# Modulation products and low halves of weights: from VectorE and GpSimd to VectorE alone, in two mixers

## The chip, the cores and the metric

The program runs on one core of a Trainium2 chip, in one launch. The metric is the device time of that launch in microseconds (us). The page and the rows below name the engines as the profiler does: PE is TensorE's matmul stream and PEld its weight loads, DVE is VectorE, ACT is ScalarE, POOL is GpSimd, and SP (SyncE) issues the loads from HBM.

## The reference, cut to what matters

Two blocks of layers work on 256 tokens of width 1024. The first has two layers, the second one; each layer is a mixer (attention or a scan) and an MLP, each followed by a normalised residual. In the first block both are modulated by vectors that a projection of the condition `c` gives:

```python
c_act = jax.nn.silu(c)
for l in range(DEPTH):                                   # 2 layers
    ada = c_act @ ada_w[l] + ada_b[l]                    # 1024 -> 6 * 1024
    sh1, sc1, g1, sh2, sc2, g2 = jnp.split(ada, 6, axis=-1)
    h = modulate(x, sh1, sc1)
    y = even_mixer(h, ...) if l % 2 == 0 else diff_mixer(h, ...)
    x = layer_norm(ALPHA * x + (1.0 + g1[:, None, :]) * y, ...)
    h = modulate(x, sh2, sc2)
    y = sq_relu_mlp(h, mlp_w1[l], mlp_w2[l])
    x = layer_norm(ALPHA * x + (1.0 + g2[:, None, :]) * y, ...)
```

`even_mixer` is the first mixer: a block-compressed attention (8 heads with compressed, selected and window keys) and a latent attention with an index score that keeps the best 64 keys. `diff_mixer` is the second. The third mixer, in the second block, joins a gated delta rule (a convolution, normalised keys, a scan over chunks of 64 tokens) and a grouped attention with 16 meta tokens. All is in float32.

## The kernel before, in words

Weights. All weights lie in one array `in_ws`, in tiles of 128 partitions by up to 1024 float32 (512 KB). Each product with a weight is made of three matmuls on halves of the mantissa, `mm3` (L385 to L389): the weight's high part `hi` is a rounded copy that ACT makes from the raw tile (`cast_hi`, L346 and L347), its low part `lo` is `raw - hi` (`cast_lo`, L349 to L352). SP issues every load, in the order of the program (`load_raw`, L333 to L337). The raw tiles stand in a ring of seven slots in both places that this change touches; SP can issue the next load once the last reader of the oldest slot is done.

Modulation. A vector of the modulation has 1024 entries, in eight parts of 128. For each part `ada_dot` (L451) loads a raw tile of 128 by 1024 on SP (L457) and needs the sum over its 1024 columns of tile times `cact`. There are two forms. With `pool` false it is one instruction of DVE, a product with a running sum (L478), and the reading of the accumulator. With `pool` "half" POOL multiplies the tile's first 512 columns by `cact` in place (L461), at the next step its other 512, and at the step after ACT runs over all 1024 columns and sums them (L474).

First mixer (`layer0`, L1036 on). Its work is a list of weight pieces (matmuls), beside a set of generators ("chains") that hold attention's steps; `weave` (L1957) goes round: each chain one step, then the casts that are due, then a piece. Three vectors of the modulation (24 dots) are one of the chains, `weave_ada` (L1070 to L1090), which starts at the 17th round and makes three steps of a dot in the POOL form and two of one in the DVE form. Here the vectors (0, 2), (0, 4) and (0, 3) are all in `spread`, so that the dots with an even part, 12 of 24, take the POOL form. In this mixer only ACT works in the order in which the program is written (`MAN[0]` is 'A'); for DVE, POOL and PE the tile scheduler sets the order.

Third mixer (`mixer2`, L2007 on). It calls the same `weave` twice. In the first call (L2029) the low part of the weights is cut by `share`, here `SHARE2` = 8: the first eight weights that the round casts have their whole low part on DVE; from the ninth on DVE makes columns 0 to 511 and POOL columns 512 to 1023. There are 11 such weights. In the second call `share` is 0, and all its weights are cut so. ACT and DVE work in written order in the first call ('AD'), in the second POOL too.

The names that come up below: `se` is a softmax tile, scaled on POOL at L1457; `ol` at L1234 are POOL's products of the compressed values; `isc` at L1163 are the index scores of the latent attention, summed over heads on DVE; `selneg` at L1189 is the mask that the selection of the best keys ends with; `C` at L2267 and `zn` at L2599 are tiles of the third mixer's scan and gate.

Of the kernel before, what the change touches and what calls it, by code (L numbers as in the profile page):

```python
# [29 lines left out]
ADA0 = 16  # L30
# [3 lines left out]
MORE1 = 2  # L34
SHARE1 = None
SHARE0 = None
SHARE2 = 8
MAN = ['A', 'ADG', 'AD', 'ADG', 'P']
EARLY = {1: "tok0", 3: "tok1", 5: "tok2", 6: "tok3"}
LAM_INIT = 0.8 - 0.6 * math.exp(-0.3)  # L40
# [226 lines left out]
class Kern:  # L267
# [768 lines left out]
    def layer0(self, stop):  # L1036
        nc, ph = self.nc, self.ph
        st = self.st = SimpleNamespace(tok=False, cmp=0, sel=0, lat=False, pc=False, scored=0)
        self.F, self.part, self.oh, self.L0 = {}, {}, None, None
        self.blk = self.T(self.acts, (128, 16, 64), "ol")  # L1040
        nc.gpsimd.memset(self.blk, 0.0)
        self.blkw = self.T(self.acts, (128, 16, 128), "oh", F32R)
        self.tok = self.T(ph, (128, 2, 416), "tok")
        self.hs = self.T(ph, (128, 256), "isc", bufs=3)
        work = []
        for n in ORDER0.split():
            f = (lambda wh, wl, i=int(n[-1]): self.tok0(i, wh, wl)) if n[:3] == "tok" else \
                (lambda wh, wl, n=n[4], i=int(n[5]): self.cmp0(n, i, wh, wl)) if n[:3] == "cmp" else \
                (lambda wh, wl, n=n: self.fm0(n, wh, wl))
            work.append((n if n[:3] == "cmp" else f"ev_{n}", None, f))  # L1050

        def begin(half):
            return half == 0 or st.scored == 4

        self.merged = set()
        work += self.out_work("ev_out", range(4), lambda k: (self.oh[:, k, :], self.ol[:, k, :]),
                              self.merged.__contains__, range(4, 4 + MORE0), begin)
        units = [self.nsa0(j) for j in range(4)] + [self.dsa0(i) for i in range(4)]
        chains = [self.loads0(), self.tok0_after(), self.compress0(), self.compressed0(), self.latent0(), self.queue(units),
                  *(self.merge0(j) for j in range(8)), self.select0(), self.weave_ada((0, 2), (0, 4), (0, 3), start=ADA0, spread=((0, 2), (0, 4), (0, 3)))]  # L1060
        self.weave(work, chains, share=SHARE0)
        self.in_order = False
        if stop == "attn0":
            for j in range(8):
                t = self.T(ph, (128, 256), "dbgo", bufs=1)
                nc.vector.tensor_add(t, self.oh[:, j, :].bitcast(F32), self.ol[:, j, :].bitcast(F32))
                self.dump(f"oT{j}", t)
        return stop != "attn0"
# [938 lines left out]
    def mixer2(self, ph, stop):  # L2007
# [7 lines left out]
        with self.banks(a=1, b=1, c=1, d=1), tc.tile_pool(name="wv", bufs=1, side="right") as wv:  # L2015
# [12 lines left out]
                      self.attn2_queries(wv, zq, aq, qT), self.delta_meta(ph, wv), att, self.gate2(wv, zz)]  # L2028
            left = self.weave(work, chains, (att,), share=SHARE2, man=2)  # L2029
        self.ctx2.enter_context(self.room(4, 3, "right"))  # L2030
# [725 lines left out]
```

## Time and profile before

| | |
|---|---|
| time, median of 3 runs | 1166.39 us (1165.0 to 1170.65) |
| the profiled execution | 1162.97 us |
| its span | 1161.2 us |
| granted clock of TensorE, mean | 0.955 |
| PE busy | 1073.1 us, 92% of the span |
| DVE busy | 840.5 us, 72% |
| ACT busy | 595.3 us, 51% |
| POOL busy | 269.3 us, 23% |
| the chain that ended last, by engine | PE 68%, DVE 14%, DMA 5%, POOL 5%, issue 4%, ACT 3% |

The first mixer lies from about 46 to 200 us of the span, the first call of `weave` in the third mixer ends at about 882 us. The shares in the table are means over stages of different kinds: the profile's 40 slices show POOL busy only in the stages of the mixers and DVE busiest in those of the first and third. "Idle before, with a releaser" in a row means that the engine stood still ahead of the instruction, and what event ended that. Busy times of one instruction include whatever it waited for once it had begun, so that the same shape can have different durations.

### The profile page before, as it was taken

What the parts mean: (1) busy time and instruction counts of PE and PEld (TensorE: products, weight loads), DVE (VectorE), ACT (ScalarE), POOL (GpSimd) and SP (SyncE); (2) the same over time, 40 slices, a digit from 0 to 9 for tenths busy, and PEclk for the clock granted to TensorE, in tenths of its full rate; (3) what the DMA queues carried; (4) which work ended last, traced back from release to release, by engine and by line L of the source; (5) the groups of instructions that cost most, each with busy time, mean ns of one, the idle gap of its engine ahead of it and who ended that gap; (6) DMA issues with size and microseconds to landing.
All of it is one profiled execution on the core that took longest, in us unless ns stands there. A gap on an engine that the chain in (4) does not pass through costs nothing.

```text
span 1161.2 us, 20465 instructions
## 1 busy us (share of the span) xinstructions
PE 1073.1 (92%) x7766; PEld 975.4 (84%) x7766; DVE 840.5 (72%) x1672; ACT 595.3 (51%) x1240; POOL 269.3 (23%) x307
## 2 busy tenths in 40 slices
PE   2789889999999999997999999998899989999996
PEld 1667667999999978896999999887776888899995
DVE  7578985799886677877976555678986677655553
ACT  2456747464445445653754444557365354544442
POOL 3284673100000201324000000336644250000000
PEclk9799888999999989997999999899899997999998
DMA  9977643299996227636587553032120252765621
GB/s 344 316 266 271 210 155 112 89 404 349 331 336 229 97 90 294 211 135 235 202 287 237 183 179 119 1 109 92 55 66 27 92 200 68 252 189 182 189 83 37
DMA packets 60447, 212.58 MB, mean 183 GB/s; under 512 B 6619, under 2 KB 9084, under 8 KB 60348
## 3 DMA queue, kind: packets, MB, share of 16 engines
q1 hardware_dynamic: 59424, 209.43, 51.3%
q0 software_dynamic: 192, 0.79, 0.4%
q8 instruction: 61, 1.00, 0.3%
q10 hardware_dynamic: 732, 1.05, 0.3%
q14 instruction: 38, 0.31, 0.1%
HBM read 209.15 MB, written 1.84 MB: 182 GB/s over the span
## 4 chain that ended last, share of the span: by engine, by line
PE 68%; DVE 14%; DMA 5%; POOL 5%; issue 4%; ACT 3%; POOLq 0%; DVEq 0%; ACTq 0%; SPq 0%
PE y L387 10%; PE y L388 10%; PE y L389 10%; PE pj L387 7%; PE pj L389 7%; PE pj L388 7%; DMA raw<-in_ws 3%; PE tr L392 2%; DVE lo L352 2%; PE y L401 2%; DVE raw L478 1%; PE y L392 1%; PE pj L392 1%; DVE cva L2178 1%; POOL se L1457 1%
## 5 line engine op out<-in xcount | busy, mean ns | idle before, releaser
L366 DVE TENSOR_TENSOR lo<-raw,hi 128x1024 fp32r<-128x1024 f32 (+1 forms) x208 | 226.6, 1105 | 107.0 <-ACT hi L365 106.9
L365 ACT ACTIVATE hi<-raw 128x1024 fp32r<-128x1024 f32 (+1 forms) x208 | 195.3, 959 | 94.1 <-PE pj L388 76.4
L387 PE MATMUL pj<-hh,hi 128*128 128x256 f32 x768 | 216.7, 282 | 0.3
L388 PE MATMUL pj<-hl,hi 128*128 128x256 f32 x768 | 216.6, 282 | 0.2 <-DVE hl L611 0.2
L389 PE MATMUL pj<-hh,lo 128*128 128x256 f32 x768 | 215.7, 281 | 0.0
L352 DVE TENSOR_TENSOR lo<-raw,hi 128x1024 fp32r<-128x1024 f32 (+2 forms) x103 | 126.6, 1236 | 42.2 <-ACT hi L347 40.8
L387 PEld LDWEIGHTS pj<-hh,hi 128*128 128x128 f32 x768 | 145.1, 189 | 2.5 <-ACT relu L807 0.9
L388 PEld LDWEIGHTS pj<-hl,hi 128*128 128x128 f32 x768 | 144.9, 189 | 1.6 <-DVE hl L611 0.4
L389 PEld LDWEIGHTS pj<-hh,lo 128*128 128x128 f32 x768 | 145.2, 189 | 0.0
L388 PE MATMUL y<-actl,hi 128*128 128x256 f32 x512 | 144.3, 282 | 0.8 <-DVE actl L810 0.7
L387 PE MATMUL y<-acth,hi 128*128 128x256 f32 x512 | 144.0, 281 | 0.0
L389 PE MATMUL y<-acth,lo 128*128 128x256 f32 x512 | 143.7, 281 | 0.0
L352 POOL TENSOR_TENSOR lo<-raw,hi 128x512 fp32r<-128x512 f32 (+3 forms) x28 | 47.5, 1703 | 357.9 <-ACT hi L347 335.9
L347 ACT ACTIVATE hi<-raw 128x1024 fp32r<-128x1024 f32 (+2 forms) x107 | 110.8, 1043 | 27.1 <-DMA raw<-in_ws 16.1
L478 DVE CUSTOM_DVE_ANT_0 raw<-raw,cact 128x1024 f32<-128x1024 f32 x75 | 97.1, 1303 | 2.7 <-DMA raw<-in_ws 2.7
L388 PEld LDWEIGHTS y<-actl,hi 128*128 128x128 f32 x512 | 96.9, 189 | 1.5 <-DVE actl L810 1.4
L387 PEld LDWEIGHTS y<-acth,hi 128*128 128x128 f32 x512 | 97.1, 190 | 0.1
L389 PEld LDWEIGHTS y<-acth,lo 128*128 128x128 f32 x512 | 96.8, 189 | 0.0
L388 PE MATMUL y<-hl,hi 128*128 128x256 f32 x296 | 84.5, 286 | 0.0
L387 PE MATMUL y<-hh,hi 128*128 128x256 f32 x264 | 79.7, 302 | 3.9 <-ACT f L1588 2.2
L809 ACT ACTIVATE acth<-act 128x256 fp32r<-128x256 f32 x96 | 39.4, 416 | 83.5 <-DVE act L808 83.5
L389 PE MATMUL y<-hh,lo 128*128 128x256 f32 x264 | 76.8, 291 | 0.0
(658 smaller groups left out, 2486.3 us busy)
## 6 DMA issues: line engine op xcount, KB each, us to landing
raw<-in_ws SPq DMA_DIRECT2D x372, 512.0 KB, 4.7
bm<-bscr SPq DMA_DIRECT2D x4, 512.0 KB, 14.6
raw<-in_ws SPq DMA_DIRECT2D x4, 416.0 KB, 8.7
bm<-in_ws SPq DMA_DIRECT2D x3, 512.0 KB, 8.2
raw<-in_ws SPq DMA_DIRECT2D x3, 408.0 KB, 3.7
zn<-in_ws SPq DMA_DIRECT2D x2, 512.0 KB, 6.6
xa<-in_xT SPq DMA_DIRECT2D x2, 512.0 KB, 6.6
oh<-in_ws SPq DMA_DIRECT2D x2, 512.0 KB, 7.3
```

Of the source, the lines that this page charges most:

```text
L347: return self.nc.scalar.activation(w[1], w[0], AF.Copy)
L352: return eng.tensor_tensor(w[2][:, a:b], w[0][:, a:b], w[1][:, a:b].bitcast(F32), op=OP.subtract)
L365: i = nc.scalar.activation(hi[:, a:b], raw[:, a:b], AF.Copy)
L366: j = (lo_by or nc.vector).tensor_tensor(lo[:, a:b], raw[:, a:b], hi[:, a:b].bitcast(F32), op=OP.subtract)
L387: mm(out, lh, rh, start=start, stop=False, skip_group_check=True)
L388: mm(out, lh, rl, start=False, stop=False, skip_group_check=True)
L389: mm(out, ll, rh, start=False, stop=stop, skip_group_check=True)
L392: self.nc.tensor.matmul(out, l, r, start=start, stop=stop, skip_group_check=True)
L401: last = self.nc.tensor.matmul(out, l, r, start=start, stop=stop, skip_group_check=True)
L478: nc.vector.tensor_tensor_reduce(out=raw, in0=raw, in1=self.cact, op0=OP.mult, op1=OP.add, scale=0.5, scalar=0.0, accum_out=t)
L809: nc.scalar.activation(ah, f, AF.Copy)
L1457: nc.gpsimd.tensor_scalar(es[g][:, sl], es[g][:, sl], sm[:, tb, g:g + 1], 1.0, op0=OP.mult, op1=OP.mult)
```

## The change

Two lines are changed. `SHARE2` becomes `None`, which `weave` reads as "no weight is cut": the 11 weights of the first call in the third mixer have their whole low part on DVE, in one instruction of 128 by 1024. And `weave_ada` is called without `spread`, whose default is empty: all 24 dots of the first mixer take the DVE form.

```diff
-SHARE2 = 8
+SHARE2 = None
...
         chains = [self.loads0(), self.tok0_after(), self.compress0(), self.compressed0(), self.latent0(), self.queue(units),
-                  *(self.merge0(j) for j in range(8)), self.select0(), self.weave_ada((0, 2), (0, 4), (0, 3), start=ADA0, spread=((0, 2), (0, 4), (0, 3)))]
+                  *(self.merge0(j) for j in range(8)), self.select0(), self.weave_ada((0, 2), (0, 4), (0, 3), start=ADA0)]
```

In the instruction streams SP's order is the same. ACT loses the 12 sums of L474 and nothing else moves on it. POOL loses 24 products of L461 and 11 low halves of L352. DVE gains 12 dots of L478 with their accumulator reads, and 11 casts of L352 grow from 512 to 1024 columns.

DVE in the first mixer, about a third of the way through it: in the rows, `raw` and `lo` with a number are the tile of a weight or of a dot, `adas` the dot's result, `oh` a merge of compressed values. Before:

```order
L352 TENSOR_TENSOR lo_161_720<-raw_159_717,hi_160_719 128x1024
L1239 TENSOR_TENSOR oh_271<-ol_269,oh_271 128x16x32
L352 TENSOR_TENSOR lo_172_765<-raw_170_762,hi_171_764 128x1024
L478 ISA raw_180_817,adas_505<-raw_180_817,cact_87 128x1024
L478 ISA adas_505 128x1
L352 TENSOR_TENSOR lo_178_802<-raw_176_799,hi_177_801 128x1024
L1163 SCALAR_TENSOR_TENSOR isc_684<-hfull_683,iw_363,p_l_90_401 128x256
```

And now:

```order
L352 TENSOR_TENSOR lo_161_716<-raw_159_713,hi_160_715 128x1024
L1239 TENSOR_TENSOR oh_271<-ol_269,oh_271 128x16x32
L478 ISA raw_174_774,adas_505<-raw_174_774,cact_87 128x1024
L478 ISA adas_505 128x1
L478 ISA raw_180_809,adas_505<-raw_180_809,cact_87 128x1024
L478 ISA adas_505 128x1
L352 TENSOR_TENSOR lo_172_759<-raw_170_756,hi_171_758 128x1024
L352 TENSOR_TENSOR lo_178_795<-raw_176_792,hi_177_794 128x1024
L1163 SCALAR_TENSOR_TENSOR isc_682<-hfull_681,iw_363,p_l_90_401 128x256
```

The dot of tile 174, which POOL made before, now stands on DVE, and it and the dot of tile 180 both stand ahead of the low parts of the weights 172 and 178 and of the first index score.

POOL at the same stage, where `se` are softmax tiles and `ol` the compressed products. Before:

```order
L461 TENSOR_TENSOR raw_141_637<-raw_141_637,cact_87 128x512 x2
L1457 TENSOR_SCALAR se_538<-se_538,ssum_540 128x128
L1457 TENSOR_SCALAR se_538<-se_538,ssum_540 128x256
L1457 TENSOR_SCALAR se_539<-se_539,ssum_540 128x128
L1457 TENSOR_SCALAR se_539<-se_539,ssum_540 128x256
L1234 TENSOR_TENSOR ol_269<-c_578,p_l_90_401 64x16x15 x2
L461 TENSOR_TENSOR raw_166_738<-raw_166_738,cact_87 128x512 x2
L1234 TENSOR_TENSOR ol_269<-c_661,p_l_90_401 64x16x15 x2
L1457 TENSOR_SCALAR se_623<-se_623,ssum_625 128x128
```

And now:

```order
L1234 TENSOR_TENSOR ol_269<-c_576,p_l_90_401 64x16x15
L1457 TENSOR_SCALAR se_538<-se_538,ssum_540 128x128
L1457 TENSOR_SCALAR se_538<-se_538,ssum_540 128x256
L1457 TENSOR_SCALAR se_539<-se_539,ssum_540 128x128
L1457 TENSOR_SCALAR se_539<-se_539,ssum_540 128x256
L1234 TENSOR_TENSOR ol_269<-c_576,p_l_90_401 64x16x15
L1234 TENSOR_TENSOR ol_269<-c_659,p_l_90_401 64x16x15 x2
L1457 TENSOR_SCALAR se_621<-se_621,ssum_623 128x128
```

The two pairs of products no longer stand ahead of the softmax's scalings and of the compressed products.

DVE in the third mixer, at the ninth weight that the round casts, among steps of the scan (`Cd`, `cvo`, `tokk`). Before:

```order
L2278 TENSOR_TENSOR Cd_9400<-C_9342,bd_8910 128x256
L2183 SCALAR_TENSOR_TENSOR cvo_9382<-cvo_9382,cva_9264 128x272
L352 TENSOR_TENSOR lo_1794_9392<-raw_1792_9389,hi_1793_9391 128x512
L2255 TENSOR_TENSOR tokk_8932<-tm_9310,nkr_9349 128x256
L2249 COPY mk_8930<-cvo_9382 128x2x16
```

And now:

```order
L2278 TENSOR_TENSOR Cd_9376<-C_9318,bd_8886 128x256
L2183 SCALAR_TENSOR_TENSOR cvo_9358<-cvo_9358,cva_9240 128x272
L352 TENSOR_TENSOR lo_1794_9368<-raw_1792_9365,hi_1793_9367 128x1024
L2255 TENSOR_TENSOR tokk_8908<-tm_9286,nkr_9325 128x256
L2249 COPY mk_8906<-cvo_9358 128x2x16
```

Nothing changes place; the cast covers twice the columns, and the half on POOL is gone.

## Rows read from the trace of the kernel before

**Rows 1.** Busy time by stretch: us, PE, PEld, DVE, ACT, POOL, granted clock, DMA share, GB/s.
```profile
60.00:92.00 32.00, 27.30 (x168) 21.25 (x168) 20.98 (x35) 18.63 (x44) 26.26 (x24) 0.89 0.60 218
92.00:160.00 68.00, 62.65 (x429) 50.34 (x428) 64.33 (x169) 47.57 (x115) 39.27 (x41) 0.95 0.70 247
...
790.00:850.00 60.00, 48.44 (x362) 46.40 (x360) 56.36 (x124) 32.25 (x80) 40.09 (x47) 0.94 0.22 71
850.00:882.00 32.00, 30.14 (x209) 24.27 (x209) 25.77 (x78) 19.61 (x58) 12.64 (x16) 1.00 0.21 67
```

**Rows 2.** POOL's groups, 92 to 160 us: busy us, mean ns, idle before.
```profile
L461 POOL TENSOR_TENSOR raw<-raw,cact 128x512 f32<-128x512 f32 x14 | 24.5, 1766 | 15.6 <-DVE lo L352 6.7 <-DMA raw<-in_ws 5.5 <-DVE smin L1444 3.3
```

**Rows 3.** DVE's groups, 92 to 160 us.
```profile
L352 DVE TENSOR_TENSOR lo<-raw,hi 128x1024 fp32r<-128x1024 f32 x17 | 25.3, 1493 | 8.0 <-ACT hi L347 8.0
L478 DVE CUSTOM_DVE_ANT_0 raw<-raw,cact 128x1024 f32<-128x1024 f32 x8 | 11.5, 1434 | 0.0
L1163 DVE SCALAR_TENSOR_TENSOR isc<-hfull,iw,isc 128x256 f32<-128x256 f32 x7 | 6.3, 899 | 0.0
L1444 DVE CUSTOM_DVE_ANT_0 se<-y,bm 128x256 f32<-128x256 f32 x12 | 4.9, 412 | 0.0
...
L1163 DVE SCALAR_TENSOR_TENSOR isc<-hfull,iw,p_l 128x256 f32<-128x256 f32 x1 | 1.5, 1495 | 0.0
```

**Rows 4.** Line L1163 alone, 92 to 160 us: shortest, median and longest ns.
```profile
L1163 DVE SCALAR_TENSOR_TENSOR isc<-hfull,iw,isc x14: 338/408/1523, 97.7 to 118.8; 128x256 f32<-128x256 f32 x7, 128x128 f32<-128x128 f32 x7
```

**Rows 5.** DVE's groups, 226 to 390 us.
```profile
L366 DVE TENSOR_TENSOR lo<-raw,hi 128x1024 fp32r<-128x1024 f32 x54 | 65.4, 1221 | 16.1 <-ACT hi L365 16.1
L478 DVE CUSTOM_DVE_ANT_0 raw<-raw,cact 128x1024 f32<-128x1024 f32 x32 | 38.3, 1216 | 0.0
L478 DVE DVE_READ_ACCUMULATOR2_ANT adas<- 128x1 f32 x32 | 2.6, 80 | 0.0
```

**Rows 6.** Timeline of POOL, 69 to 112 us: start, us, instruction, idle before.
```profile
78.31 3.40 POOL L461 TENSOR_TENSOR raw<-raw,cact 128x512 f32<-128x512 f32 x2
81.67 2.46 POOL L1234 TENSOR_TENSOR ol<-c,p_l 64x240 f32<-64x240 f32 x2
...
102.87 3.74 POOL L461 TENSOR_TENSOR raw<-raw,cact 128x512 f32<-128x512 f32 x2 [5.21 <-DVE lo L352]
```

**Rows 7.** Timeline of DVE, three pieces between 84 and 160 us.
```profile
91.59 1.22 DVE L352 TENSOR_TENSOR lo<-raw,hi 128x1024 fp32r<-128x1024 f32 x1 [6.00 <-ACT hi L347]
...
103.19 4.50 DVE L352 TENSOR_TENSOR lo<-raw,hi 128x1024 fp32r<-128x1024 f32 x2
...
159.07 0.23 DVE L1189 TENSOR_SCALAR selneg<-isc 128x128 f32<-128x128 f32 x1
```

**Rows 8.** Timeline of ACT, 83 to 92 us.
```profile
84.16 0.63 ACT L1237 ACTIVATE oh<-ol 128x512 fp32r<-128x512 f32 x1 [3.69 <-POOL ol L1234]
...
89.47 1.05 ACT L474 ACTIVATE raw<-raw 128x1024 f32<-128x1024 f32 x1
```

**Rows 9.** Waits of SP, 46 to 200 us: us in total, times, longest.
```profile
SPq L336 <- ACT raw L474: 13.9, 4, 4.8
SPq L457 <- ACT raw L474: 11.3, 2, 7.5
```

**Rows 10.** DVE's and POOL's groups, 790 to 850 us.
```profile
L2267 DVE SCALAR_TENSOR_TENSOR C<-ol,beta,C 128x128 f32<-128x128 f32 x6 | 5.8, 962 | 0.2
L352 DVE TENSOR_TENSOR lo<-raw,hi 128x512 fp32r<-128x512 f32 x7 | 5.0, 713 | 0.2 <-ACT hi L347 0.2
...
L352 POOL TENSOR_TENSOR lo<-raw,hi 128x512 fp32r<-128x512 f32 x8 | 10.8, 1345 | 0.5 <-ACT hi L347 0.4
```

**Rows 11.** Timelines of POOL and DVE, 793 to 813 us.
```profile
794.71 1.28 POOL L352 TENSOR_TENSOR lo<-raw,hi 128x512 fp32r<-128x512 f32 x1
...
794.86 1.28 DVE L2267 SCALAR_TENSOR_TENSOR C<-ol,beta,C 128x128 f32<-128x128 f32 x1
...
812.61 0.35 DVE L2267 SCALAR_TENSOR_TENSOR C<-ol,beta,C 128x128 f32<-128x128 f32 x1
```

## The prediction

> **What bounds the kernel now.** I first read the busy time by stretch, since the means over the span hide the two stages that change. In the first mixer between 92 and 160 us DVE is busy 64.33 of 68.00 us and PE 62.65; in the third between 790 and 850 us DVE is busy 56.36 of 60.00 and PE only 48.44 [rows 1]. In both DVE is the engine with the least room, and POOL works beside it for 39 and 40 us. In 60 to 92 us it is otherwise: DVE 20.98 of 32.00, POOL 26.26, PE 27.30 [rows 1]. In 850 to 882 us PE has 30.14 of 32.00 and DVE 25.77 [rows 1].
>
> Then the groups, for what DVE's busy time is made of. The 17 casts of 128 by 1024 in 92 to 160 us take 1.493 us each, the 8 dots 1.434 and seven sums of index scores 0.899 [rows 3]; in a stretch where POOL does next to nothing the same casts take 1.221 and the dots 1.216 [rows 5], and the median of the index sums is 0.408 [rows 4]. So part of DVE's busy time is no work. The timelines show what it is: at 102.87 POOL runs two halves of a dot for 3.74 us, and at 103.19 two casts of DVE take 4.50 us in place of 2.44 [rows 6, 7]. The third mixer shows the same at 794.7: a half of a cast on POOL, 1.28 us, and beside it a sum of `C` on DVE of 1.28 us, which takes 0.35 at 812.61 [rows 11]. The two engines take turns: a DVE instruction that meets one of POOL's stands until that is done. Each half on POOL thus costs DVE time as well.
>
> A rule of the Trainium skill bears on how far this goes: "SBUF — State Buffer", section "Who interferes with whom", says that a DVE instruction with two SBUF inputs contends with a GpSimd one that reads SBUF, that the loser is held for the whole of the other, and that one with at most one SBUF input is left alone. The trace agrees on the last point: the softmax instruction that reads PSUM, L1444, has a mean of 0.412 us beside the same POOL work [rows 3]. If each of the 14 products of 92 to 160 us held a DVE instruction for its whole mean of 1.766 us [rows 2], 24.7 us would come back there in place of the 11 that I take below, and the forecast would be 13.7 us lower; the rows of DVE show far less, since POOL's time has its own waits for DVE in it.
>
> **The change, part by part.** *Dots in the first mixer.* Removed are 24 POOL products, 14 of them (24.5 us, [rows 2]) in 92 to 160 us, and 12 sums on ACT; added are 12 dots on DVE at 1.216 + 0.080 = 1.30 us undisturbed [rows 5], 15.6 us in all. The tile scheduler's new order puts 11 of them ahead of the last `selneg` (159.07, [rows 7]), 4 of these before 92 us. Three places.
>
> A, 92 to 160 us. DVE is nearly full, so the 7 dots there cost 7 x 1.30 = +9.1 us. What comes back is the stretching: casts 17 x (1.493 - 1.221) = 4.6, dots 8 x (1.434 - 1.216) = 1.7, index sums 7 x (0.899 - 0.408) = 3.4, the first of them 1.495 - 0.408 = 1.1 [rows 3 to 5]; 10.8 in all, and I take 11 because smaller groups hold a little more. It could be 0 if other POOL work takes the port, and no more than the 14 products' own 24.5 us; I stay at the DVE rows, as these are what DVE lost. A is 9.1 - 11.0 = -1.9 us.
>
> B, 60 to 92 us. Here the four added dots (5.2 us) lie in DVE's 11.0 idle us [rows 1]. The chain of waits runs through POOL: the products at 78.31 (3.40 us) stand ahead of the compressed products at 81.67, ACT waits 3.69 us for these at 84.16, then does the sum L474 (89.47, 1.05 us) ahead of the next weight's `hi`, and DVE stands 6.00 us for that `hi` until 91.59 [rows 6 to 8]. Without products and sum this could be earlier by 3.40 + 1.05 = 4.5 us; ends are 0 (the next link, index scores and softmax on PE, is late anyway) and -6.0, the whole idle time. I take -4. If the cover fails and the four dots hold up a cast there, B is +1 instead. ACT's other eleven sums, about 1.05 us each, are costed at nothing beside B: ACT is busy 47.57 of 68.00 us [rows 1]. In 160 to 190 us the last dot stands on an engine that waits for softmax and selection anyway, and is taken as nothing.
>
> C, *low halves in the third mixer*, 790 to 850 us. Eight of the eleven casts grow by 1.221 - 0.713 = 0.508 us: +4.1 on a DVE that is 94% busy [rows 1, 5, 10]. What returns lies between 6 x (0.962 - 0.35) = 3.7, which the sums of `C` alone show, and the eight halves' own 10.8 us on POOL [rows 10, 11]. If each half held one instruction for what the pair at 794.7 shows, 1.28 - 0.35 = 0.93, it would be 7.4; I take 6.5, so C = -2.4. The other three casts (+1.5) lie in 850 to 882 us, where DVE has 6.2 us of room and PE sets the pace [rows 1]: nothing. A low half that is whole is ready on one engine later than two halves side by side by up to 0.5 us; PE is idle 11.6 of 60 us there, so a matmul that waits for it is possible, and is in the range.
>
> No SP issue moves in order. SP waited 13.9 + 11.3 = 25.2 us for L474 to free a tile [rows 9]; a dot on DVE frees it in one step and not three. I give that no price of its own, since loads run ahead where DVE is behind.
>
> The sum: -1.9 - 4.0 - 2.4 = -8.3 us on the profiled execution's 1162.97 (span 1161.2 and 1.8 around it): 1154.7. The median of the runs shown, 1166.39, lies 3.4 above that execution, and so the predicted time is 1158.1 us.
>
> **The rivals.**
>
> *Slower: the port's time is not returned, and the dots stand ahead of the weights.* In the new order the dots of tiles 174 and 180 both go before the low parts of weights 172 and 178, for which PE waits. DVE then carries 9.1 us more in A and 4.1 in C, 13.2 in all, against r times 17.5 (11 + 6.5) returned. With r under 0.75 the change is a loss, under 0.42 one of over 5.8 us (0.5%, about what a measurement of this kernel can tell from no change). For it: POOL keeps its softmax scalings and products of the compressed values, about 39.27 - 24.5 = 15 us of work in 92 to 160, and 29 us in 790 to 850 [rows 1, 2, 10], which can meet the longer casts; an instruction of DVE that no longer meets a dot may meet one of those. Against: those are there before too and were counted before. At r = 0.3 it is 13.2 - 5.3 = +7.9: 1174.3 us. A page gives this rival's rule: the Trainium skill, "Perfetto Trace Analysis", section "Optimizing Scalar/DVE Operations", holds that where DVE is saturated, moving work off to ScalarE or even GpSimd may make sense, by which taking the help away costs time; it adds itself that the two share a read port, so that it might not help. The trace bears out the addendum more than the rule, as the 4.50 us at 103.19 show [rows 7].
>
> *Little: DVE's gain is not on the path.* PE is busy 62.65 of 68.00 in A [rows 1], so that a DVE which is 2 us earlier may only meet a PE that is not, and in B the scalings and the matrix products of the compressed attention may be bound by something else than POOL. What remains is C at half and nothing else, about -1.5: 1164.9 us. For it: DVE is 14% of the chain that ended last and PE 68%. Against: DVE stood for the wait in B, and in C PE has 11.6 us of idle time.
>
> *Larger: slots come free earlier.* The whole idle time of 6.0 us goes in B, and the loads, which SP held 25.2 us for L474 [rows 9], land so early that the casts between 92 and 160 us are never late for DVE; -6.0 in B, -4.5 in A, -2.5 in C, or -13.0: 1153.4 us. For it: 8.0 us of DVE's idle time in A end with ACT's `hi` [rows 3]. Against: DVE, not the loads, is the full engine there.
>
> That the change doesn't do what it says is not a rival that I give a chance: the order shows all POOL products gone.
>
> **How the numbers follow.** Forecast 0.36, little 0.30, slower 0.20, larger 0.14. The forecast's own range is 1154 to 1161. Faster by over 0.5% (below 1160.6) holds the larger case and all of the forecast's but a tail: 0.14 + 0.33 = 0.47. Within 0.5% (to 1172.2) holds the little case and that tail, 0.30 + 0.03 = 0.33. Slower by over 0.5% holds the slower rival, 0.20. The range of 8 in 10 runs from 1152.0, which leaves out the far half of the larger case, to 1173.5, which leaves out the worse half of the slower one.
>
> **What the profile after would show.** No L461. In the first mixer the casts back at 1.22 to 1.30 us and the dots near 1.22 (A); if both stay above 1.4, the port went to other POOL work and the slower rival holds. DVE's 6.00 us before 91.59 at 2 or below, and the following stage earlier by some 4 us (B). SP without waits on L474. The last `selneg` at 154 or before; if it is at 157 or later with casts at 1.22, the path was another engine's. In the third mixer `C` at 0.35 to 0.6 instead of 0.962, and the stretch that took 60.0 us some 2 to 3 us shorter (C); if `C` is short and the stretch as long, PE or the scan's own chain bound it. Wrong outright would be a first mixer that ends later than before.

## The result and the profile after

The changed kernel takes 1154.55 us (median of 16 runs, 1151.41 to 1166.05); the kernel before, run beside it, 1168.85 (16 runs). The ratio is 0.9893, with a 95% interval of 0.9868 to 0.9918: 12.5 us faster, within 9.6 to 15.4. The profiled execution took 1151.99 us against 1162.97, 11.0 less.

Busy time by stretch, columns as in [rows 1]; the third mixer runs some 5 to 11 us earlier now, so its two stretches are shifted:

```profile
60.00:92.00 32.00, 26.61 (x176) 21.53 (x175) 24.73 (x47) 16.95 (x40) 17.29 (x16) 0.95 0.70 258
92.00:160.00 68.00, 62.93 (x452) 51.39 (x451) 60.85 (x184) 38.91 (x99) 18.30 (x27) 0.97 0.74 247
...
785.00:839.00 54.00, 46.42 (x350) 44.81 (x349) 50.60 (x120) 30.33 (x75) 30.52 (x39) 0.94 0.24 78
839.00:871.00 32.00, 30.35 (x211) 24.70 (x211) 27.02 (x78) 19.91 (x57) 7.48 (x13) 1.00 0.23 67
```

DVE in 92 to 160 us is 3.5 us less busy, although it issues 184 instructions in place of 169. Its groups there show why (they answer to [rows 3]):

```profile
L352 DVE TENSOR_TENSOR lo<-raw,hi 128x1024 fp32r<-128x1024 f32 x16 | 19.9, 1244 | 3.1 <-ACT hi L347 3.1
L478 DVE CUSTOM_DVE_ANT_0 raw<-raw,cact 128x1024 f32<-128x1024 f32 x15 | 18.2, 1213 | 0.0
...
L1163 DVE SCALAR_TENSOR_TENSOR isc<-hfull,iw,isc 128x256 f32<-128x256 f32 x7 | 3.4, 483 | 0.0
```

The 15 dots take 1.213 us each where 8 took 1.434, the casts 1.244 for 1.493, the index sums 0.483 for 0.899. The sums of `C` in the third mixer are back as well [rows 10]:

```profile
L2267 DVE SCALAR_TENSOR_TENSOR C<-ol,beta,C 128x128 f32<-128x128 f32 x6 | 2.1, 351 | 0.2
```

Where in the program the time went is read from matmuls, which are the same 7766 in both kernels: the time between the ends of the same matmuls, at 46, 92, 160 and 200 us of the profile before, and for the third mixer at 780 and 885. "Again" is the changed kernel profiled a second time, the last two columns each have one part of the change.

| us | before | after | again | first mixer's part alone | third mixer's part alone |
|---|---|---|---|---|---|
| 46 to 92 | 45.96 | 43.88 | 44.58 | 44.23 | 48.20 |
| 92 to 160 | 67.99 | 65.61 | 65.96 | 65.65 | 67.50 |
| 160 to 200 | 39.98 | 38.32 | 38.37 | 38.96 | 39.98 |
| 780 to 885 | 104.98 | 100.31 | 107.84 | 108.56 | 103.49 |

In the first mixer the three executions with dots on DVE agree within 1.1 us, and lie 5.0 to 6.1 us below the kernel before (7.9 at most, against the old code in the last column). The third mixer is not to be read from one execution: the same code takes 100.31 and 107.84 us. The two profiles differ there in TensorE's granted clock. Near the end of the stage, after:

```profile
842.00:846.00 4.00, 3.30 (x21) 2.87 (x22) 3.93 (x12) 2.54 (x5) 0.78 (x1) 1.00 0.40 128
846.00:850.00 4.00, 3.56 (x30) 3.00 (x28) 3.62 (x10) 1.32 (x5) 0.00 (x0) 1.00 0.03 9
850.00:854.00 4.00, 3.98 (x26) 3.54 (x27) 3.30 (x13) 2.49 (x6) 1.44 (x3) 1.00 0.45 131
```

and the same matmuls in the same kernel again:

```profile
844.00:848.00 4.00, 3.02 (x19) 2.47 (x18) 3.70 (x8) 3.37 (x9) 0.56 (x1) 0.90 0.08 15
848.00:852.00 4.00, 4.00 (x17) 3.71 (x17) 2.49 (x10) 0.30 (x1) 0.20 (x1) 0.50 0.35 122
852.00:856.00 4.00, 4.00 (x21) 3.80 (x19) 2.85 (x8) 1.32 (x5) 0.00 (x0) 0.50 0.00 0
856.00:860.00 4.00, 4.00 (x14) 2.95 (x15) 1.88 (x5) 0.00 (x0) 0.00 (x0) 0.50 0.39 131
```

For 12 us the clock is granted at 0.50, the lower of its two levels (1.2 GHz), after PE had been busy 3.02 of 4.00 us, and PE then has no idle time at all. In the first profile it is 1.00 (2.4 GHz) over these matmuls. So the size of the third mixer's gain is taken from the timed runs. The traces agree with them on the direction: the seven whose third mixer is the changed one (the others' edits lie in the first mixer) take 100.3 to 103.7 us there and once 107.8, the three with the old code 105.0, 108.6 and 108.6.

### The profile page after: what moved, and what is told of

Its sections match the earlier page's. It is cut to its first block, busy times and chain, and to the rows that moved or that the text cites. A ratio compares the mean times of both kernels' runs of the same rounds, so it can differ in the third digit from the quotient of the medians.

```text
span 1150.2 us, 20384 instructions
## 1 busy us (share of the span) xinstructions
PE 1066.6 (93%) x7766; PEld 973.5 (85%) x7766; DVE 834.6 (73%) x1696; ACT 583.0 (51%) x1216; POOL 221.9 (19%) x272
## 4 chain that ended last, share of the span: by engine, by line
PE 46%; DVE 9%; POOL 3%; issue 3%; ACT 2%; DMA 1%; POOLq 0%; DVEq 0%; ACTq 0%; SPq 0%
PE y L387 7%; PE y L388 6%; PE y L389 6%; PE pj L387 5%; PE pj L388 5%; PE pj L389 5%; DVE lo L352 2%; PE tr L392 2%; PE y L401 2%; PE y L392 1%; PE sc L392 1%; DVE cva L2178 1%; PE d L392 1%; POOL se L1638 1%; DMA raw<-in_ws 1%
## 5 line engine op out<-in xcount | busy, mean ns | idle before, releaser
L352 DVE TENSOR_TENSOR lo<-raw,hi 128x1024 fp32r<-128x1024 f32 (+2 forms) x103 | 126.3, 1233 | 43.6 <-ACT hi L347 42.3
L478 DVE CUSTOM_DVE_ANT_0 raw<-raw,cact 128x1024 f32<-128x1024 f32 x87 | 108.5, 1255 | 2.9 <-DMA raw<-in_ws 2.9
L352 POOL TENSOR_TENSOR lo<-raw,hi 128x512 fp32r<-128x512 f32 (+3 forms) x17 | 32.6, 1933 | 358.4 <-ACT hi L347 349.4
```

The lines of the kernel that those rows point to most:

```text
L352: return eng.tensor_tensor(w[2][:, a:b], w[0][:, a:b], w[1][:, a:b].bitcast(F32), op=OP.subtract)
L478: nc.vector.tensor_tensor_reduce(out=raw, in0=raw, in1=self.cact, op0=OP.mult, op1=OP.add, scale=0.5, scalar=0.0, accum_out=t)
```

## The experiments

The theory was that a POOL instruction that reads SBUF holds up a DVE one with two SBUF inputs, and that this time is what the change gives back. The rivals were POOL's queue, ACT's sums and the release of the tiles, and, for the size, that DVE is not on the path. Every ratio below is to the kernel before, run beside the run in question.

**Each part alone.** The first mixer's part:

```diff
-SHARE2 = None
+SHARE2 = 8
```

> The first mixer's edit alone: all 24 dots on DVE, the third mixer's low halves cut as before. Theory (the stretching of DVE by POOL's products goes away, place by place): the matmuls run 0.6 us late at 46 us in the profile after and 5.4 us early at the end of the first mixer, so this kernel shows the same 5 to 6 us by 200 us and keeps it to the end, ratio to before about 0.995. Rival (the two edits help each other, or the gain of the first stage is given back at a later load): under 3 us at the end. Rival (the saving is all the third mixer's): 0.

Measured: ratio 0.9938 (0.9917 to 0.9959), 7.2 us. The third mixer's part is the kernel before with `SHARE2 = None`.

> The third mixer's edit alone. Theory: nothing before 780 us, then the 4.6 us that the profile after gains between 790 and 880 us, ratio to before about 0.996; the sums of C at L2267 back near 0.35 to 0.6 us. With the first part's 5 to 6 us it adds up to the 11 us of the whole. Rival (the 4.6 us come from a better start that the first mixer's edit gives, by loads or the granted clock): under 2 us.

Measured: 0.9954 (0.9925 to 0.9983), 5.4 us, with C at 0.352 us. The two sum to 12.6 us, the whole is 12.5: nothing shows that the parts help or hinder each other, though the intervals of the two leave room for a few us. In the profile of the first part the third mixer seems to give back 3.6 us, but its code there is that of the kernel before, and the granted clock differs (0.92 on average, 0.97 before); the timed runs show no such loss.

**What the added dots cost.** In the changed kernel 12 dots are left out. The diff is against the code of before, with `spread` given and `SHARE2 = None`, so that the first branch of `weave_ada` is the edited one; e5 and e6 below are made in the same way:

```diff
-                    rest = self.ada_dot(*lv, m, d[:, m:m + 1], "half")
+                    raw = self.load_raw("ada%d%d%d" % (*lv, m)); nc.vector.tensor_copy(d[:, m:m + 1], raw[:, 0:1])
...
-                    rest(1)
+                    pass
...
-                    rest()
+                    pass
```

> The changed kernel, but 12 of the 24 dots of the first mixer are left out (the tiles are loaded and one column is copied), on POOL and on DVE. It gives the price of the added dots on DVE. Theory (DVE sets the pace of 92 to 160 us): 7 dots of 1.30 us there, so the end of the first mixer 6 to 9 us earlier than in the changed kernel, ratio to before about 0.982. Rival (PE or the chain over softmax sets it, and DVE has room since the stretching is gone): 0 to 3 us, ratio about 0.988.

Measured: 0.9859 (0.9827 to 0.9891), about 4 us below the changed kernel; in the profile the first mixer is 5.2 us shorter (142.60 against 147.81), 2.8 of it in 92 to 160. That lies between theory and rival. DVE gave up 15.6 us of dots and the stage a third of it, since PE is there as well:

```profile
92.00:160.00 68.00, 64.49 (x456) 51.58 (x455) 55.25 (x191) 38.86 (x99) 21.57 (x34) 0.97 0.71 240
```

**ACT's sums.** The kernel before with short sums:

```diff
-                    nc.scalar.activation(raw, raw, AF.Copy, scale=0.5, accum_out=t)
+                    nc.scalar.activation(raw[:, :8], raw[:, :8], AF.Copy, scale=0.5, accum_out=t)
```

> The kernel before, with ACT's 12 sums of the dots cut from 1024 columns to 8 (the rest of the sum is left out), POOL's products as before. It tells ACT's time from POOL's. Theory (the port and POOL's queue are what cost): at most 1 to 2 us earlier than before, ratio 0.998 to 1.000, casts and dots on DVE still near 1.5 us in 92 to 160 us. Rival (the sum on ACT stands ahead of the casts' high parts and holds the tiles): 4 us or more, ratio about 0.996 or below.

Measured: 1.0029 (1.0003 to 1.0055). The sums fell from 1.052 to 0.202 us each and nothing was gained; the casts stay at 1.55 us. It is even 3 us slower, for which no run has a cause: the first mixer takes 155.52 us in its profile, as the old code does in the run of the third part alone (155.68). ACT's work and the earlier release by a microsecond are not where the gain is.

**Reading against writing.** POOL makes the products over again in the changed kernel, after DVE's dot of the tile (e5), as in the diff; in e6 `nc.gpsimd.memset(raw, 0.0)` stands in the place of each product:

```diff
-                    rest = self.ada_dot(*lv, m, d[:, m:m + 1], "half")
+                    raw = self.raw(); self.ada_dot(*lv, m, d[:, m:m + 1], False, raw)
                     yield
-                    rest(1)
+                    nc.gpsimd.tensor_tensor(raw[:, :512], raw[:, :512], self.cact[:, :512], op=OP.mult)
                     yield
-                    rest()
+                    nc.gpsimd.tensor_tensor(raw[:, 512:], raw[:, 512:], self.cact[:, 512:], op=OP.mult)
```

> The changed kernel, and POOL makes its 24 half products of the first mixer over again on the 12 tiles, after DVE's dot of the tile (results unused). Against the next kernel, which has memsets in the same places, only the reading of SBUF differs. Theory (a POOL instruction that reads SBUF holds up a DVE one with two SBUF inputs): casts and dots of 92 to 160 us back to 1.4 to 1.6 us, some 11 us of stretching there on a full DVE, the end of the first mixer 8 to 14 us later than in the changed kernel; ratio to before 1.000 to 1.005. Rival (what costs is POOL's queue and the later release of the tiles): 0 to 4 us later, and the same as with memsets.

> The changed kernel, and POOL sets each of the 12 tiles to zero twice (128x1024 each) after DVE's dot, at the places of the products: it only writes SBUF. Theory: casts and dots stay at 1.22 to 1.30 us, and the first mixer ends 0 to 3 us later than in the changed kernel (POOL's queue alone); ratio to before 0.989 to 0.992. Rival (any POOL work there slows DVE): casts and dots above 1.4 us and as late as with products.

Measured: with products 1.0043 (1.0016 to 1.0070), 17 us above the changed kernel; with memsets 0.9910 (0.9875 to 0.9944), no difference from it. The first mixer takes 163.91 us with products and 147.86 with memsets. DVE in 92 to 160 us with products (the matmuls of this stage run later there, from 98 to 170 us, where the casts take 1.372 and the dots 1.400):

```profile
L352 DVE TENSOR_TENSOR lo<-raw,hi 128x1024 fp32r<-128x1024 f32 x15 | 20.7, 1381 | 7.3 <-ACT hi L347 7.3
L478 DVE CUSTOM_DVE_ANT_0 raw<-raw,cact 128x1024 f32<-128x1024 f32 x12 | 17.2, 1432 | 0.0
```

and with memsets:

```profile
L352 DVE TENSOR_TENSOR lo<-raw,hi 128x1024 fp32r<-128x1024 f32 x17 | 21.1, 1240 | 8.4 <-ACT hi L347 8.3
L478 DVE CUSTOM_DVE_ANT_0 raw<-raw,cact 128x1024 f32<-128x1024 f32 x15 | 18.2, 1211 | 0.0
```

POOL's own groups (46 to 215 us with products, 46 to 200 with memsets) show the other half (busy us, mean ns, idle before). With products:

```profile
L1084 POOL TENSOR_TENSOR raw<-raw,cact 128x512 f32<-128x512 f32 x12 | 21.2, 1766 | 0.0
```

With memsets of twice the columns:

```profile
L1084 POOL MEMSET raw<- 128x1024 f32 x12 | 11.4, 953 | 0.7
```

The memsets stand in the same queue, write the same tiles and cost nothing that the runs can tell; what costs is the products, which read. The page of the Trainium skill weighed before ("SBUF — State Buffer", section "Who interferes with whom") excepts a GpSimd instruction that only writes; the memsets bear that out. (Its point on DVE instructions with at most one SBUF input leaves out DVE's two-port modes, which the prediction's wording does not.) What the pair does not separate is how much of the 16 us is DVE waiting for POOL and how much POOL for DVE, since a product occupies POOL's queue for longer, 1.26 us at the shortest, and longer still when it is held.

**The same in the third mixer.** After each of the 11 casts POOL makes the half over again (e7), as in the diff; in e9 it does `nc.gpsimd.memset(x[0], 0.0)` instead:

```diff
-                        self.cast_lo(x, nc.vector)
+                        self.cast_lo(x, nc.vector); man == 2 and n > 8 and nc.gpsimd.tensor_tensor(x[0][:, 512:], x[0][:, 512:], x[1][:, 512:].bitcast(F32), op=OP.subtract)
```

> The changed kernel, and in the third mixer POOL makes the 11 half low parts over again, out into the raw tile (unused). DVE's whole casts stay. Theory: C at L2267 and the other DVE work is stretched by 6 to 8 us again in the third mixer, where DVE is full, and the time is 4 to 8 us above the changed kernel: ratio to before 0.993 to 0.996. Rival (what the edit took away was PE's wait for POOL's half, which no matmul needs here): 0 to 2 us above.

> The changed kernel, and in the third mixer POOL sets each of the 11 raw tiles to zero (128x1024) after DVE's cast, in the places where the run e7 had POOL read them: the same wait at the head of POOL's queue, no reading. Theory (e7's loss was the held-up DVE): 0 to 3 us above the changed kernel, ratio to before 0.989 to 0.992. Rival (e7's loss was POOL's queue, since its extra instructions waited 22.8 us for DVE's casts ahead of the scan's own POOL steps): 6 us or more above, ratio 0.995 to 0.999, as in e7.

Measured: reading 0.9982 (0.9954 to 1.0009), 10 us above the changed kernel and more than the theory gave; writing 0.9919 (0.9892 to 0.9947), 2 to 3 us above it. The wait for DVE's cast at the head of POOL's queue is in both, 22.8 us of it with halves and 20.2 with memsets. POOL's waits in the third mixer (us in total, times, longest), with halves:

```profile
POOL raw L1991 <- DVE lo L352: 22.8, 6, 7.4
```

and with memsets:

```profile
POOL raw L1991 <- DVE lo L352: 20.2, 6, 5.2
```

so it is no more than 3 us of the loss, and some 7 us come with the reading. DVE accounts for about half of these. Between the same matmuls, from 780 to 885 us of the profile before, with halves and then with memsets:

```profile
775.49:889.86 114.37, 103.94 (x643) 93.92 (x643) 97.55 (x227) 61.36 (x163) 60.70 (x69) 0.84 0.21 65
776.59:879.81 103.22, 93.13 (x644) 84.05 (x643) 93.73 (x227) 61.33 (x163) 56.95 (x69) 0.93 0.23 72
```

DVE is busy 3.8 us more with the reading. The other difference is the granted clock, 0.84 against 0.93, by which the same matmuls keep PE busy 10.8 us longer in these two profiles; over the whole span of the timed runs it is 0.950 against 0.954. Whether the held-up DVE brought the clock down, or these executions merely differ in it, no run tells.

**Can more be had?** Three tries on the changed kernel. The second call of the third mixer whole as well (`share=None` there):

> The changed kernel with the second call of the third mixer whole as well: 8 more weights have their low part on DVE alone, none on POOL. In that stage of the changed kernel PE is busy 56.2 of 58.0 us and DVE 38.1. Theory (a gain is to be had only where DVE is full): the same as the changed kernel within 1.5 us, ratio to before about 0.989. Rival (taking POOL's halves away helps everywhere): 3 us or more below it, ratio about 0.986. Rival (a whole cast is late for PE): 1 to 4 us above.

Measured: 0.9899 (0.9861 to 0.9936), the same. Next, three more kinds of POOL products of the third mixer on DVE (`nc.gpsimd` to `nc.vector` at L2256, L2483 and L2611):

> The changed kernel with three more kinds of POOL products of the third mixer on DVE (L2256, L2483, L2611: ten of 128x512 and two of 128x128), from which the remaining stretching there comes in the main (5.1 us of the 8.3 by comparing each DVE instruction with the shortest of its shape). Theory (a product on POOL costs a full DVE as much as it would take on DVE): ten at 0.70 us and two at 0.35 added, 5 us or so returned, so within 2 us of the changed kernel; ratio to before 0.987 to 0.991. Rival (as with the cut casts, the stage gains more than DVE's sum, since the scan's steps no longer queue on POOL): 3 us or more below it, ratio about 0.986 or less.

Measured: 0.9907 (0.9877 to 0.9936), the same, as the theory had it. The changed kernel ran again beside it:

> The changed kernel again, on the same chip as the two runs with it, so that they can be set against it: ratio to before 0.987 to 0.992 as measured, and a second profile, which tells how much of a stage's time differs from one execution to another: the theory has the first mixer within 1 us of the first profile and the third within 3.

Measured: 0.9900 (0.9867 to 0.9933). The first mixer repeats (148.91 against 147.81, a little over the 1 us expected), the third does not (7.5 us apart, not 3). Last, the softmax scalings on ACT:

```diff
-                nc.gpsimd.tensor_scalar(es[g][:, sl], es[g][:, sl], sm[:, tb, g:g + 1], 1.0, op0=OP.mult, op1=OP.mult)
+                nc.scalar.activation(es[g][:, sl], es[g][:, sl], AF.Copy, scale=sm[:, tb, g:g + 1])
```

> The changed kernel with the 48 softmax scalings of the first mixer (L1457) on ACT in place of POOL. In the changed kernel four of them take 4.98 us at 80.45, between DVE's dots, where the run without the added dots shows 2.95 and the kernel before 2.06; the whole group of 48 is 31.1 us on POOL. Theory (POOL's scalings and DVE's dots hold each other up, and ACT has room: 38.9 of 68.0 us busy in 92 to 160): 46 to 92 us shorter by 1 to 3 us, the first mixer's end 2 to 6 us earlier than in the changed kernel, ratio to before 0.984 to 0.988. Rival (ACT works in written order, so that a scaling that waits for DVE's reciprocal holds up the high parts of the weights queued behind it): first mixer 3 us or more later, ratio 0.993 or above.

Measured: 0.9893 (0.9865 to 0.9921), no gain. The profile shows one and where it goes. From 46 to 160 us the stage is 2.7 us shorter (106.78 against 109.49), from 160 to 200 it is 6.6 longer (44.91 against 38.32; the granted clock there is 0.77, in the changed kernel 0.87). ACT's idle time ahead of the scalings, in 46 to 200 us, is of the kind that the rival named:

```profile
L1457 ACT ACTIVATE se<-se,ssum 128x128 f32<-128x128 f32 x24 | 9.5, 396 | 12.8 <-DVE ssum L1454 9.2 <-DVE ssum L1452 3.6
```

The first mixer as a whole is 3.9 us longer in this profile, which the timed runs do not show as a loss. None of the three tries beats the changed kernel.

## Why the prediction was right, point by point

The direction and the mechanism held, and the rivals "slower" and "little" fell. The size was too small: 8.3 us forecast, 12.5 measured. The time, 1154.55 us, lies at the lower edge of the forecast's own range and nearer to the larger rival's 1153.4 than to 1158.1; which terms were too small, and which too large, follows.

*A, the dots against the stretching in 92 to 160 us.* Forecast -1.9, profile -2.0 to -2.4. The casts and the dots came back within 0.03 us of the undisturbed rows, as the term assumed. The index sums were read too low: 0.408 us is a median over two shapes [rows 4], and the shape that the term prices takes 0.483 undisturbed, so that 2.9 us and not 3.4 were theirs to return. Still r, the share of the port's time that is returned, is near 1 and not 0.3: by comparing each DVE instruction with the short ones of its shape (the tenth percentile), the stretching within this stage fell from 12.4 to 0.4 us. The agreement is luck in part. Between the same matmuls DVE is busy 5.6 us less than the 64.33 of before [rows 1], not 1.9:

```profile
90.66:156.26 65.60, 61.50 (x435) 50.47 (x435) 58.75 (x178) 39.58 (x100) 16.71 (x25) 0.97 0.73 244
```

Six of the added dots fall there, not seven, and more came back than the term took. Against that the term counted a microsecond of DVE as one of the stage, while the run without the added dots shows it to be worth about a third; a third of 5.6 is 1.9. In the reading run it is worth more: the first mixer lost 16 us for some 14 us of stretching more than with memsets, but POOL's own steps are held there as well.

*B, 60 to 92 us.* Forecast -4, profile -1.4 to -2.1; the term was too large by half or more. The first link did what was said: ACT waits 1.03 us for POOL's `ol`, not 3.69 [rows 8], and does that merge at 80.27 instead of 84.16. The next link, which the step named only as the end of its range ("is late anyway"), then took half of this back. POOL's timeline after (start, us, instruction, idle before):

```profile
80.45 4.98 POOL L1457 TENSOR_SCALAR se<-se,ssum 128x128 f32<-128x128 f32 x4 [0.22 <-DVE ssum L1454]
```

PE's:

```profile
82.20 0.33 PE L1464 MATMUL tr<-p_first,se 128*128 128x128 f32 x1 [2.05 <-POOL se L1457]
84.69 1.49 PE L1464 MATMUL tr<-p_first,se 128*128 128x128 f32 x5 [2.03 <-POOL se L1457]
```

ACT's:

```profile
80.27 0.63 ACT L1237 ACTIVATE oh<-ol 128x512 fp32r<-128x512 f32 x1 [1.03 <-POOL ol L1234]
85.41 0.49 ACT L1466 ACTIVATE sT<-tr 128x384 f32<-128x384 f32 x1 [4.51 <-PE tr L1464]
```

And DVE's:

```profile
81.92 1.30 DVE L478 CUSTOM_DVE_ANT_0 raw<-raw,cact 128x1024 f32<-128x1024 f32 x1
...
83.15 1.22 DVE L478 CUSTOM_DVE_ANT_0 raw<-raw,cact 128x1024 f32<-128x1024 f32 x1
...
89.62 1.23 DVE L352 TENSOR_TENSOR lo<-raw,hi 128x1024 fp32r<-128x1024 f32 x1 [5.24 <-ACT hi L347]
```

The four scalings took 2.06 us in the kernel before and 4.98 now, since DVE's dots run beside them; PE's transposes wait for these, ACT for the transposes, and DVE still stands 5.24 us for `hi`. In the run without the added dots the same four take 2.95:

```profile
79.27 2.95 POOL L1457 TENSOR_SCALAR se<-se,ssum 128x128 f32<-128x128 f32 x4 [0.22 <-DVE ssum L1454]
```

So the added dots were not hidden in DVE's idle time, as the step put it: each engine is held by the other, and POOL was on the path. The run without them is 2.2 us shorter over these matmuls (41.69 us).

*160 to 190 us, taken as nothing.* Profile -1.0 to -1.7 for 160 to 200. In the kernel before, the last dot's two products ran on POOL, a dot of DVE took 2.34 us beside them, and POOL's next mask for the selection waited for `smin`, which DVE makes after that dot:

```profile
161.89 3.46 POOL L461 TENSOR_TENSOR raw<-raw,cact 128x512 f32<-128x512 f32 x2
161.89 2.34 DVE L478 CUSTOM_DVE_ANT_0 raw<-raw,cact 128x1024 f32<-128x1024 f32 x1
166.39 0.45 POOL L1431 TENSOR_TENSOR bsel<-bm,selneg 128x128 f32<-128x128 f32 x1 [1.04 <-DVE smin L1444]
```

In the kernel after, this mask does not wait:

```profile
161.28 0.46 POOL L1431 TENSOR_TENSOR bsel<-bm,selneg 128x128 f32<-128x128 f32 x1
```

The step asked what the added dot costs there and not what the removed products had held up. It was not the order in POOL's queue, for POOL had stood for 1.04 us when `smin` came. Part of the gain may be the granted clock, 0.87 in the two executions with 1.6 and 1.7 us, 0.82 in the one with 1.0 and 0.83 before.

*C, the third mixer.* Forecast -2.4, timed -5.4 with an interval from -8.8 to -2.0 that just holds the forecast. What was sized too small is what returns. The whole third mixer between the same matmuls, before and after:

```profile
780.06:885.04 104.98, 90.76 (x643) 80.63 (x642) 94.55 (x228) 61.63 (x164) 60.31 (x70) 0.97 0.22 71
774.77:875.08 100.31, 90.29 (x644) 80.95 (x643) 90.72 (x227) 61.38 (x163) 46.85 (x58) 0.97 0.23 74
```

DVE's low parts take 16.0 us now (13 whole) where they took 10.1 (two whole and 11 halves), and yet DVE is busy 3.8 us less. So 9.7 us came back, where the term took 6.5. DVE's busy time repeats, unlike the stage's: 91.17 us in the second profile, 90.97 in the run of the third part alone. How many of the 5.4 us are DVE's, and how many come with the granted clock, stays open.

*The larger rival's loads.* SP no longer waits for L474, as forecast, but it waits elsewhere: for DVE's casts, 38.6 us in 46 to 200 us (17.7 in the kernel before), and for the dots' results 10.9 (4.0). All its waits there sum to 129.4 us, 135.0 before. Waits of SP after:

```profile
SPq L336 <- DVE lo L352: 20.6, 8, 4.2
SPq L457 <- DVE lo L352: 18.0, 7, 8.1
```

The size of that rival's gain (13.0) came out nearly right by a way that was wrong: SP waited for tiles nearly as long as before.

*The mark chosen.* The last `selneg` was to show A: at 154 or before if it held, while 157 or later with short casts would put the path on another engine. It is at 158.11, and yet the matmuls there are 3.8 us ahead: the scheduler now places it behind one more cast and 11 more dots. A single instruction is a poor mark; the matmuls were the better one.

## What to carry to other kernels

Before work is split between DVE and POOL, set the DVE instructions beside it against the same shape where POOL is quiet: here 14 half products on POOL went with 12.0 us of stretching on a full DVE, where the seven whole dots that they replaced take 9.1. Then ask what DVE's time is worth at the end, which was a third where PE was nearly as full. Count the hold both ways, since a POOL step on the critical chain is stretched too, as the four scalings were from 2.06 to 4.98 us. And take the same stage of the same code from two executions before a difference of a few microseconds there is explained.

## What the runs showed that was not expected

POOL's memsets left DVE's casts at 1.240 us in the first mixer, as expected, but in the third DVE is busy 3.0 us more with them than in the changed kernel (93.73 us), for which no run has a cause. A change that takes work off POOL is easily given back: all three tries moved work without moving the end, and for the scalings on ACT a gain had been expected. And the third mixer differed by 7.5 us between two executions of one kernel, with a mean granted clock of 0.97 in one and 0.89 in the other; their totals are 1151.99 and 1164.08 us.
